# FFN down products issued in threes between the pair products

## The chip, the cores and the metric

The kernel runs on one core of one Trainium2 chip. The metric is the device time of one launch, in microseconds. TensorE is named PE (its weight loads PEld), VectorE DVE, ScalarE ACT, GpSimd POOL, and SyncE, which issues the loads, SP.

## The reference, cut to what matters

One transformer block on 512 tokens of 1024 features: a feed-forward network (FFN), an attention mixer, a second FFN, and a last norm. The change touches both FFNs alone.

```python
def swiglu(h, w_gate, w_up, w_down):
    return (jax.nn.silu(h @ w_gate) * (h @ w_up)) @ w_down

x = x + 0.5 * swiglu(rmsnorm(x, norm_ffn1[l]), w_ffn1_gate[l], w_ffn1_up[l], w_ffn1_down[l])
x = x + hybrid_mixer(rmsnorm(x, norm_mix[l]), ...)
x = x + 0.5 * swiglu(rmsnorm(x, norm_ffn2[l]), w_ffn2_gate[l], w_ffn2_up[l], w_ffn2_down[l])
```

`w_gate` and `w_up` are 1024 x 2816, `w_down` is 2816 x 1024, all float32.

## The kernel before, in words

Every matrix is held as a sum of a high and a low half, and every product of two 128-blocks is made of three matmuls (high by high, high by low, low by high): `mm3`, lines 100 to 103. In a trace each `mm3` is one row of L101, one of L102 and one of L103. The halves of a weight are made by ACT (high, L92 or L233) and DVE (low, L96 or L234).

An FFN has 22 feature blocks `f` of 128. The first four are computed plainly (`plain`, products called `pgu`). The other 18 are computed in nine pairs by a scheme with seven products instead of eight on half-width operands (`pair`, line 304). A pair has 14 steps: seven products (`u`, `v` or `w`) for gate and for up. A step is four `mm3` with 256 columns each, so 12 matmuls (`pu`, `pv`, `pw` in the trace). Each step needs a sum of weight tiles (L319, some steps), a high half (L233) and a low half (L234). Behind a step follow small sums out of PSUM (L339 to L365).

The products with `w_down` (`down`, line 385) go by groups of four feature blocks: for each of the eight output blocks `d`, four `mm3` with 512 columns, 12 matmuls called `pd`, accumulate in one PSUM bank, and `half_added` (L507, DVE) adds the half of it to `x[d]`. The down products of a group of four are laid between the pair steps of the next group of four (`mixed`, line 419): after about every fourth pair step, one block of 12 `pd` matmuls. The down products of the first, plain group stand ahead of the pairs, in two batches of four output blocks. The last group (two feature blocks, `f` 20 and 21) has 14 pair steps, between which seven of the eight blocks of `f` 16 to 19 lie, the eighth behind them. After it the first FFN has the down products of its last two feature blocks (`wd1b`), and the second FFN goes on with transposes of `x` (`px`) and the last products.

`go` (line 442) walks the list of steps in order. It issues a step's loads 12 steps ahead, its weight sums 6 ahead, its halves 4 ahead. The walk gives the order by priority; a list scheduler with a simulated timeline then fixes each engine's order, and may pass an instruction whose inputs are late in its simulation. `tc.issue_after(ins)` makes the instructions in its block stand behind `ins` on that engine's queue.

PSUM has eight banks, in four tags (`s`, `t`, `o`, `mm`) of two. `u` uses `s`, `v` uses `t`, `w` uses `o`; the blocks of down products between pairs use `mm`; the first group's down products take the tags in rotation (`pt` with tag `None`, line 48).

Of the kernel before, what the change touches and what calls it, by code (L numbers as in the profile page):

```python
# [18 lines left out]
NK = D // 128  # L19
NF = F // 128  # L20
NT = S // 128
FP = 4
# [7 lines left out]
def block_kernel(ctx: ExitStack, tc: tile.TileContext, A: dict, out: bass.AP):  # L30
# [7 lines left out]
    nc = tc.nc  # L38
# [9 lines left out]
    def pt(tag, name):  # L48

        if tag is None:  # L50
            tag = ("s", "t", "o", "mm")[turns[0] % 4]
            turns[0] += 1
        return ps.tile([128, S], F32, name=name, tag=tag, bufs=2)
# [46 lines left out]
    def mm3(p, w, v, first, last, again=False):  # L100
        nc.tensor.matmul(p, w[0], v[0], start=first, stop=False, skip_group_check=again)  # L101
        nc.tensor.matmul(p, w[0], v[1], start=False, stop=False, skip_group_check=again)  # L102
        nc.tensor.matmul(p, w[1], v[0], start=False, stop=last, skip_group_check=again)  # L103

    def mm2(p, w, v, first, last):

# [10 lines left out]
    for k in range(NK):  # L117
        x = xp.tile([128, S], F32, name=f"x{k}")
# [73 lines left out]
    class Ffn:  # L192
# [14 lines left out]
        def __init__(self, wg, wu, which, tmp, hp, sp):  # L207
            self.w, self.which, self.tmp, self.hp, self.sp = (wg, wu), which, tmp, hp, sp
            self.xg, self.hs, self.steps = None, {}, []
            self.b, self.temps = {}, {}  # L210
            self.last_lo = None
            self.x_made = None
            self.rms_at = {}
            self.th, self.tl = [sp.tile([128, 4, 3, HT], F32R, name=n, tag=n, bufs=1) for n in ("th3", "tl3")]
            sp.tile([128, 16], F32, name="gap", tag="gap", bufs=1)
# [88 lines left out]
        def pair(self, f):  # L304

            A, half, bank, part, out = {}, {}, {}, {}, {}
# [22 lines left out]
            def run(m, to, a, b, first):  # L329
                if first:  # L330
                    bank[m, to] = ps.tile([128, S], F32, name="p" + to, tag={"u": "s", "v": "t", "w": "o"}[to],
                                          bufs=2)[:, :HT]
                hi, lo = half.pop((m, a))
                for k, x in enumerate(self.moving(b)):
                    mm3(bank[m, to], (hi[:, k], lo[:, k]), x, first and k == 0, k == 3, not first)

            def copied(m, to, name):
                part[m, name] = self.sp.tile([128, HT], F32, name="wc", tag="wc", bufs=4)
# [43 lines left out]
                                  lambda m=m, then=then: then(m)])  # L382
            return steps

        def down(self, w, fs, then, tag="mm", groups=(1,) * NK, kept_back=True):

            n = len(fs)
            raw, got, bank = {}, {}, {}

            def loads(d):  # L390
                if d % (8 // n) == 0:
                    raw[d * n // 8] = chunk((8, 128))
                    fetch(raw[d * n // 8], w[d * n // 8])

            def halves_of(d):
                if d % (4 // n) == 0:
                    i = d * n % 8
                    with self.behind_lo() if kept_back else nullcontext():
                        parts = halves(raw[d * n // 8][:, i:i + 4])
                    for k, v in enumerate(parts):  # L400
                        got[d + k // n, k % n] = v

            def run(d):
                ds = {sum(groups[:g]): range(sum(groups[:g]), sum(groups[:g + 1])) for g in range(len(groups))}.get(d)
                if ds is None:
                    return
                for i in ds:
                    bank[i] = pt(tag, "pd")
                for ks in ([range(n)] if len(ds) == 1 else [range(n - 1), range(n - 1, n)]):
                    for i in ds:  # L410
                        for k in ks:
                            mm3(bank[i], got[i, k], self.hs[fs[k]], k == 0, k == n - 1)
                for i in ds:
                    then(i, bank[i])

            return [[lambda d=d: loads(d), None, lambda d=d: halves_of(d), lambda d=d: run(d), None, True]
                    for d in range(NK)]

        def mixed(self, steps, fills, tail=1):

# [8 lines left out]
        def lay(self, wd):  # L429

            for f in range(FP):
                self.steps += self.plain(f)
            self.steps += self.down(wd[0], range(FP), half_added, None, (4, 4), False)
            fills = []
            for f in range(FP, NF, FP):
                fs = range(f, min(f + FP, NF))
                pairs = [step for i in fs[::2] for step in self.pair(i)]
                self.steps += self.mixed(pairs, fills) if fills else pairs
                if len(fs) == FP:
                    fills = self.down(wd[f // FP], fs, half_added)  # L440

        def go(self, after):
            steps, at = self.steps, [0, 0, 0]
            late, count = None, 0
            for i, s in enumerate(steps):
                for j, ahead in enumerate((12, 6, 4)):
                    while at[j] < min(i + ahead + 1, len(steps)):
                        if steps[at[j]][j]:
                            steps[at[j]][j]()
                        at[j] += 1  # L450
                down = len(s) == 6
                if down and late:
                    late()
                s[3]()
                if not down:
                    if late:
                        late()
                    if i == 2 * FP - 1:
                        s[4]()
                        s[4] = None  # L460
                    after(count)
                    count += 1
                late = s[4]
            if late:
                late()


    scr_t = dp.tile([16, 128, RVW], F32, name="scr_t")
# [40 lines left out]
    with ExitStack() as ph:  # L509
        tmp = ph.enter_context(tc.tile_pool(name="tmp1", bufs=5))  # L510
        hp = ph.enter_context(tc.tile_pool(name="hp1", bufs=2))
        sp = ph.enter_context(tc.tile_pool(name="sp1", bufs=2))


        wake = pt(None, "wake")
        for _ in range(12):
            nc.tensor.matmul(wake.rearrange("p (a b) -> p a b", a=4), ones,
                             ones.unsqueeze(1).to_broadcast([128, 4, 128]), start=True, stop=True)
        nc.scalar.activation(R[:, 0:1], eps, AF.Sqrt)
        ffn = Ffn(A["wg1"], A["wu1"], 0, tmp, hp, sp)  # L520
        ffn.xg = [gained(k, 0) for k in range(NK)]
        ffn.x_made = made[0]
        ffn.rms_at = {(1, 0, 4): summed, (1, 1, 0): turned_R}

        make_rows = bias_rows(hp)

        def after(i):
            if i == 0:
                with tc.issue_after(ffn.first_up.ins):
                    for k in range(NK):  # L530
                        squares(hp, k, "h", 16)
                rms(None)
            if i == 3:
                make_rows()
            if 3 <= i < 7:
                ffn.sums_of_x(i - 3)
            if i == 7:
                for k in range(4):
                    ffn.blocks_of_x(k)
            if 20 <= i < 60 and i % 5 == 0:  # L540
                h = slice(2 * (i // 5) - 8, 2 * (i // 5) - 6)
                row = scr_r[h]
                with behind_fetched():
                    nc.sync.dma_start(scr_t[h].rearrange("h p w -> p h w"),
                                      bass.AP(tensor=row.tensor, offset=row.offset,
                                              ap=[[0, 128], [RVW, 2], [1, RVW]]))
            if i >= 70 and i % 8 == 0 and (i - 72) // 8 < 8:
                a = (i - 72) // 8
                row = scr_c[0:1, :]
                with behind_fetched():  # L550
                    for j in range(NT):
                        nc.sync.dma_start(
                            cb[a * 16:(a + 1) * 16, j],
                            bass.AP(tensor=row.tensor, offset=row.offset + 31 - 8 * j - a,
                                    ap=[[CMW, 16], [16 * CMW, 8], [1, 32]]))

        xg = []

        def then(d, p):
            if d == 0:  # L560
                with tc.issue_after(ffn.silu.ins):
                    nc.scalar.activation(rc[:, 0:1], eps, AF.Sqrt)
            half_added(d, p)
            xg.append(gained(d, 1))
            squares(tmp, d, "tmp", 5)

        ffn.lay(A["wd1a"])
        ffn.steps += ffn.down(A["wd1b"], range(NF - NF % FP, NF), then, None, (4, 2, 2))
        ffn.go(after)


    with ExitStack() as ph:
# [12 lines left out]
        got = {}  # L585
# [637 lines left out]
```

## Time and profile before

| | us |
|---|---|
| median of 3 runs | 998.72 (997.28 to 998.82) |
| profiled execution, its own time | 999.69 |
| its span, first to last instruction | 997.9 |
| PE busy | 979.2 (98%), 6084 matmuls |
| PEld busy | 870.7 (87%) |
| DVE busy | 780.9 (78%) |
| ACT busy | 566.3 (57%) |
| mean granted PE clock | 0.997 |

The pair stages of the two FFNs lie at about 70 to 340 us and 700 to 972 us of the span. Rows of a timeline carry a start and a duration, both in us; matmuls are pipelined, so a row's duration is longer than the time to the next row's start, and it is the distance of starts that adds up to the span.

### The profile page before, as it was taken

How to read it: one execution, taken by the hardware profiler on the slowest of the kernel's cores; microseconds unless marked ns; L12 is line 12 of the kernel's file. 1: busy time of each engine (PE TensorE's matmuls, PEld its weight loads, DVE VectorE, ACT ScalarE, POOL GpSimd, SP SyncE). 2: the span in 40 equal slices, each digit the busy share in tenths (PEclk: the TensorE clock that was granted, in tenths of full speed). 3: DMA queues.
4: the chain of work that ended last, by engine and by line, in shares of the span. 5: the costliest groups of instructions: out<-in, count | busy, mean ns of one | idle time of the engine just before them, and what ended most of it. 6: DMA issues, size and time to landing. Idle time of an engine off the chain costs nothing.

```text
span 997.9 us, 16910 instructions
## 1 busy us (share of the span) xinstructions
PE 979.2 (98%) x6084; PEld 870.7 (87%) x6084; DVE 780.9 (78%) x1579; ACT 566.3 (57%) x1165; POOL 132.6 (13%) x176
## 2 busy tenths in 40 slices
PE   9999999999999999999999999999999999999996
PEld 6789999999999898787877888888998999999995
DVE  6996987687777587768788978889788787777854
ACT  6464655454544365567687886656456455444426
POOL 0000000000000000035666666100000000000002
PEclk9999999999999999999999999999999999999999
DMA  7345544332321136531221232135343322341102
GB/s 258 104 172 175 190 128 132 109 98 82 108 66 50 51 97 186 171 114 33 61 62 54 80 86 79 64 99 197 89 165 114 118 78 76 127 127 43 54 11 85
DMA packets 50057, 104.52 MB, mean 105 GB/s; under 512 B 10130, under 2 KB 14691, under 8 KB 49973
## 3 DMA queue, kind: packets, MB, share of 16 engines
q1 hardware_dynamic: 49684, 102.91, 33.1%
q8 instruction: 48, 0.79, 0.3%
q10 hardware_dynamic: 288, 0.52, 0.1%
q14 instruction: 37, 0.30, 0.1%
HBM read 97.98 MB, written 5.30 MB: 103 GB/s over the span
## 4 chain that ended last, share of the span: by engine, by line
PE 92%; DVE 4%; ACT 1%; DMA 1%; issue 1%; SPq 0%; ACTq 0%; DVEq 0%
PE pd L101 8%; PE pd L102 8%; PE pd L103 8%; PE pu L101 6%; PE pu L103 6%; PE pu L102 6%; PE pw L101 5%; PE pw L102 4%; PE pw L103 4%; PE pp L103 3%; PE pgu L101 3%; PE pgu L102 3%; PE pp L101 3%; PE pgu L103 3%; PE pp L102 3%; PE pv L101 3%
## 5 line engine op out<-in xcount | busy, mean ns | idle before, releaser
L233 ACT ACTIVATE sph<-aw 128x512 fp32r<-128x512 f32 x252 | 157.7, 630 | 158.6 <-PE pu L102 74.6
L92 ACT ACTIVATE whi<-raw 128x512 fp32r<-128x512 f32 (+1 forms) x200 | 122.1, 621 | 174.7 <-PE pd L102 88.4
L234 DVE TENSOR_TENSOR spl<-aw,sph 128x512 fp32r<-128x512 f32 x252 | 170.8, 686 | 56.6 <-ACT sph L233 53.2
L102 PE MATMUL pd<-h,whi 128*128 128x512 f32 x336 | 131.5, 391 | 0.0
L96 DVE TENSOR_TENSOR wlo<-raw,whi 128x512 fp32r<-128x512 f32 (+1 forms) x168 | 111.2, 672 | 25.8 <-ACT whi L92 22.2
L103 PE MATMUL pd<-h,wlo 128*128 128x512 f32 x336 | 130.5, 389 | 0.0
L101 PE MATMUL pd<-h,whi 128*128 128x512 f32 x336 | 129.3, 392 | 0.0
L101 PE MATMUL pu<-th,sph 128*128 128x256 f32 x432 | 121.2, 281 | 0.0
L103 PE MATMUL pu<-th,spl 128*128 128x256 f32 x432 | 121.1, 280 | 0.0
L102 PE MATMUL pu<-tl,sph 128*128 128x256 f32 x432 | 121.1, 280 | 0.0
L319 DVE TENSOR_TENSOR aw<-aw 128x512 f32<-128x512 f32 x144 | 98.2, 683 | 0.0
L507 DVE SCALAR_TENSOR_TENSOR x<-pd,x 128x512 f32<-128x512 f32 x88 | 59.8, 685 | 40.2 <-PE pd L103 39.3
L102 PEld LDWEIGHTS pu<-tl,sph 128*128 128x128 f32 x432 | 82.0, 190 | 1.2
L101 PEld LDWEIGHTS pu<-th,sph 128*128 128x128 f32 x432 | 81.5, 189 | 1.1
L103 PEld LDWEIGHTS pu<-th,spl 128*128 128x128 f32 x432 | 81.2, 188 | 0.0
L101 PE MATMUL pw<-xo,sph 128*128 128x256 f32 x288 | 80.7, 281 | 0.0
L102 PE MATMUL pw<-xo,sph 128*128 128x256 f32 x288 | 80.5, 280 | 0.0
L103 PE MATMUL pw<-xo,spl 128*128 128x256 f32 x288 | 79.7, 280 | 0.0
L103 PEld LDWEIGHTS pd<-h,wlo 128*128 128x128 f32 x336 | 63.1, 188 | 12.9
L102 PEld LDWEIGHTS pd<-h,whi 128*128 128x128 f32 x336 | 63.3, 189 | 10.7
L101 PEld LDWEIGHTS pd<-h,whi 128*128 128x128 f32 x336 | 63.1, 188 | 11.0
L102 PEld LDWEIGHTS pw<-xo,sph 128*128 128x128 f32 x288 | 54.9, 190 | 1.1
(246 smaller groups left out, 2445.8 us busy)
## 6 DMA issues: line engine op xcount, KB each, us to landing
aw<-in_wg SPq DMA_DIRECT2D x72, 256.0 KB, 3.3
aw<-in_wu SPq DMA_DIRECT2D x72, 256.0 KB, 4.5
raw<-in_wd1a SPq DMA_DIRECT2D x20, 512.0 KB, 4.0
raw<-in_wd2a SPq DMA_DIRECT2D x20, 512.0 KB, 5.2
raw<-in_w_a SPq DMA_DIRECT2D x16, 512.0 KB, 4.5
raw<-in_w SPq DMA_DIRECT2D x8, 512.0 KB, 4.1
raw<-in_w_o SPq DMA_DIRECT2D x8, 512.0 KB, 3.5
raw<-in_wg SPq DMA_DIRECT2D x7, 512.0 KB, 4.0
```

The costliest lines, as they stand in the source:

```text
L92: last_hi[0] = nc.scalar.activation(hi, v, AF.Copy)
L96: nc.vector.tensor_tensor(lo, v, f32(hi), ALU.subtract)
L101: nc.tensor.matmul(p, w[0], v[0], start=first, stop=False, skip_group_check=again)
L102: nc.tensor.matmul(p, w[0], v[1], start=False, stop=False, skip_group_check=again)
L103: nc.tensor.matmul(p, w[1], v[0], start=False, stop=last, skip_group_check=again)
L233: nc.scalar.activation(hi, v, AF.Copy)
L234: self.last_lo = nc.vector.tensor_tensor(lo, v, f32(hi), ALU.subtract)
L319: nc.vector.tensor_tensor(to, x, y, op)
L507: nc.vector.scalar_tensor_tensor(xs[d], p, 0.5, xs[d], ALU.mult, ALU.add)
```

## The change

A block of down products between pair steps is no longer issued as 12 matmuls in a row. It is taken apart into four `mm3` (triples), which go to a list `waiting`. After each pair step one triple is issued; a second one goes into the middle of the step if more than four wait. Each triple's matmuls are ordered behind the last pair matmul issued so far (`in_pair`) with `issue_after`. `half_added` follows the block's last triple. Of the first group's down products, ahead of the pairs, all but the last triple are issued as before; the last one waits, and a counter `held` keeps it back for the first five pair steps and lets it out at the end of the sixth. The PSUM tags of that first group are now fixed by output block (`s`, `t`, `o`, `mm`). What still waits when the steps are over is issued in a row. `wd1b` keeps its order.

```diff
     def mm3(p, w, v, first, last, again=False):
...
-        nc.tensor.matmul(p, w[1], v[0], start=False, stop=last, skip_group_check=again)
+        return nc.tensor.matmul(p, w[1], v[0], start=False, stop=last, skip_group_check=again)
...
+            self.waiting = []
+            self.in_pair = None
+            self.held = 5
...
                 for k, x in enumerate(self.moving(b)):
-                    mm3(bank[m, to], (hi[:, k], lo[:, k]), x, first and k == 0, k == 3, not first)
+                    self.in_pair = mm3(bank[m, to], (hi[:, k], lo[:, k]), x, first and k == 0, k == 3, not first)
+                    if k == 1:
+                        self.between(self.held == 0 and len(self.waiting) > 4)
+                self.between(self.held == 0)
+                self.held = max(self.held - 1, 0)
...
-        def down(self, w, fs, then, tag="mm", groups=(1,) * NK, kept_back=True):
+        def down(self, w, fs, then, tags=("mm",), groups=(1,) * NK, kept_back=True, left=None):
...
-                for i in ds:
-                    bank[i] = pt(tag, "pd")
+
+                def triple(i, k):
+                    if k == 0:
+                        bank[i] = pt(tags[i % len(tags)], "pd")
+                    with tc.issue_after(self.in_pair.ins) if left != 0 and self.in_pair else nullcontext():
+                        mm3(bank[i], got[i, k], self.hs[fs[k]], k == 0, k == n - 1)
+                    if k == n - 1:
+                        then(i, bank[i])
+
+                todo = []
                 for ks in ([range(n)] if len(ds) == 1 else [range(n - 1), range(n - 1, n)]):
-                    for i in ds:
-                        for k in ks:
-                            mm3(bank[i], got[i, k], self.hs[fs[k]], k == 0, k == n - 1)
-                for i in ds:
-                    then(i, bank[i])
+                    todo += [lambda i=i, k=k: triple(i, k) for i in ds for k in ks]
+                at = 0 if left is None else len(todo) - (left if ds[-1] == NK - 1 else 0)
+                if at:
+                    self.between(len(self.waiting))
+                for one in todo[:at]:
+                    one()
+                self.waiting += todo[at:]
...
+        def between(self, n):
+
+            for _ in range(min(n, len(self.waiting))):
+                self.waiting.pop(0)()
...
-            self.steps += self.down(wd[0], range(FP), half_added, None, (4, 4), False)
+            self.steps += self.down(wd[0], range(FP), half_added, ("s", "t", "o", "mm"), (4, 4), False, 1)
...
             if late:
                 late()
+            self.between(len(self.waiting))
...
-        ffn.steps += ffn.down(A["wd1b"], range(NF - NF % FP, NF), then, None, (4, 2, 2))
+        ffn.steps += ffn.down(A["wd1b"], range(NF - NF % FP, NF), then, (None,), (4, 2, 2), left=0)
```

## Rows read from the trace of the kernel before

**Rows 1.** The page: the span, and each engine's busy time, share and instructions.
```profile
span 997.9 us, 16910 instructions
PE 979.2 (98%) x6084; PEld 870.7 (87%) x6084; DVE 780.9 (78%) x1579; ACT 566.3 (57%) x1165; POOL 132.6 (13%) x176
```

**Rows 2.** Stretches of the pair stages: length, busy time (instructions) by engine, granted clock.
```profile
core 0: us, PE busy (x) PEld busy (x) DVE busy (x) ACT busy (x) POOL busy (x), PEclk, DMA share, GB/s
141.25:339.72 198.47, 198.47 (x1369) 184.74 (x1368) 148.66 (x257) 95.13 (x179) 0.00 (x0) 1.00 0.29 86
773.60:972.07 198.47, 198.47 (x1369) 184.74 (x1368) 148.67 (x257) 93.66 (x177) 0.00 (x0) 1.00 0.25 79
700.60:753.90 53.30, 52.20 (x409) 50.52 (x408) 41.68 (x75) 27.49 (x56) 0.00 (x0) 1.00 0.38 119
```

**Rows 3.** The same stretch, PE's instructions that write `pd` alone.
```profile
141.25:339.72 198.47, 81.80 (x337) 1.00 0.29 86
```

**Rows 4.** Timeline of PE: a block, 72 pair matmuls, the next block (first of each).
```profile
144.09 0.40 PE L101 MATMUL pd<-h,whi 128*128 128x512 f32 x1
...
146.83 0.28 PE L101 MATMUL pv<-xo,sph 128*128 128x256 f32 x1
...
155.31 0.40 PE L101 MATMUL pd<-h,whi 128*128 128x512 f32 x1
```

**Rows 5.** Timeline of PE: two down matmuls, 44 pair matmuls, a block (first of each).
```profile
133.50 0.40 PE L101 MATMUL pd<-h,whi 128*128 128x512 f32 x1
...
133.97 0.28 PE L101 MATMUL pu<-th,sph 128*128 128x256 f32 x1
...
138.97 0.40 PE L103 MATMUL pd<-h,wlo 128*128 128x512 f32 x1
```

**Rows 6.** Groups by line, 141.25 to 339.72 us: busy us, mean ns of one.
```profile
L101 PE MATMUL pu<-th,sph 128*128 128x256 f32 x152 | 42.7, 281 | 0.0
```

**Rows 7.** The same view, 134.0 to 138.96 us.
```profile
L101 PE MATMUL pu<-th,sph 128*128 128x256 f32 x8 | 2.2, 277 | 0.0
```

**Rows 8.** Timeline: three down matmuls, 16 pair matmuls, the next down (first of each).
```profile
125.14 0.40 PE L102 MATMUL pd<-h,whi 128*128 128x512 f32 x1
...
125.84 0.28 PE L102 MATMUL pw<-xo,sph 128*128 128x256 f32 x1
...
127.66 0.40 PE L102 MATMUL pd<-h,whi 128*128 128x512 f32 x1
```

**Rows 9.** Timeline: four down, seven pair, one down, pair (first of each).
```profile
121.57 0.40 PE L103 MATMUL pd<-h,wlo 128*128 128x512 f32 x1
...
122.50 0.28 PE L101 MATMUL pw<-xo,sph 128*128 128x256 f32 x1
...
123.33 0.39 PE L101 MATMUL pd<-h,whi 128*128 128x512 f32 x1
123.56 0.28 PE L103 MATMUL pw<-xo,spl 128*128 128x256 f32 x1
```

**Rows 10.** Timeline: six pair, two down, 18 pair, then down (first of each).
```profile
700.57 0.28 PE L101 MATMUL pu<-xo,sph 128*128 128x256 f32 x1
...
701.28 0.40 PE L101 MATMUL pd<-h,whi 128*128 128x512 f32 x1
...
701.75 0.28 PE L101 MATMUL pu<-xo,sph 128*128 128x256 f32 x1
...
703.79 0.40 PE L103 MATMUL pd<-h,wlo 128*128 128x512 f32 x1
```

**Rows 11.** Timeline of PE: around its one stop in the second FFN's pairs.
```profile
749.62 0.28 PE L103 MATMUL pv<-xo,spl 128*128 128x256 f32 x1
751.00 0.39 PE L101 MATMUL pu<-xo,sph 128*128 128x256 f32 x1 [1.10 <-ACT t L361]
```

**Rows 12.** Timeline of ACT, same stretch.
```profile
749.01 0.63 ACT L92 ACTIVATE whi<-raw 128x512 fp32r<-128x512 f32 x1 [3.93 <-DMA raw<-in_wd2a]
```

**Rows 13.** Waits, 141.25 to 339.72 us: us in total, times, longest us.
```profile
ACT whi L92 <- PE pd L102: 39.7, 29, 2.1
DVE x L507 <- PE pd L103: 15.1, 12, 2.9
```

## The prediction

> **What bounds the kernel now.** The page comes first: PE is busy 979.2 of 997.9 us [rows 1]. Such a share can hide a slow issue, so the second view is the table of stretches. In 141.25 to 339.72 us PE is busy for all of 198.47 us, at a granted clock of 1.00, while DVE is busy 148.66 us and ACT 95.13 us; the second FFN's stretch has the same 198.47 us [rows 2]. So in these two stretches nothing but PE's own pace sets the time, and the change removes no matmul. The only stop above 1 us in the pair stages is at 749.62 us [rows 11].
>
> What can still move is how far apart PE starts its matmuls, so the third view is the timeline of PE, read by distances of starts. From 146.83 to 155.31 us there are 72 pair matmuls, 8.48 / 72 = 117.8 ns each [rows 4]. From 133.97 to 138.97 us there are 44 of the same shape, 5.00 / 44 = 113.6 ns each [rows 5]. The same product has two paces. The groups by line show it as well: one L101 `pu` takes 281 ns on average in the long stretch and 277 ns in the short one [rows 6, 7]. In both long stretches the pace is the slow one throughout.
>
> What decides between them, in this trace, is the run of `pd` matmuls just before. Behind a block of 12 the pace is slow [rows 4]. Behind two `pd` it is fast [rows 5], also where it was slow before: 6 pair matmuls in 0.71 us (118 ns), two `pd`, then 18 in 2.04 us (113.3 ns) [rows 10]. Behind three `pd` it is fast, 16 in 1.82 us (113.8 ns) [rows 8]. Behind four it is slow, 7 in 0.83 us (118.6 ns), and the next single `pd` leads to the fast pace again [rows 9]. I went through all such runs in both pair stages: 12 have one to three `pd` (three of one, six of two, three of three), and a fast pace follows each; 69 have four or more, and a slow pace follows each, six of them although it was fast before. What is not in the trace: three `pd` with a slow pace before them. All three cases of three came from the fast pace.
>
> **The change part by part.** The list of steps puts four triples into `waiting` at every fourth pair step, and each pair step lets one out at its end. So PE should see 12 pair matmuls, 3 `pd`, 12 pair matmuls and so on, with the second triple in the middle of a step only where more than four wait (at the turn of a group of four, and in all of the last 14 steps).
>
> *Pace of the pair matmuls.* Each long stretch holds 1369 PE instructions, 337 of them `pd` [rows 2, 3]; one `pd` is the tail of the block before, so 336 `pd` and 1032 pair matmuls. By triples all of these follow a run of three, so they go at 113.6 instead of 117.8 ns: 2 x 1032 x 4.2 ns = 8.7 us less. Check of the sum: 1032 x 117.8 ns = 121.6 us, and 198.47 - 121.6 = 76.9 us for 336 `pd`, 228.9 ns each, which agrees with 2.74 us / 12 = 228 ns of a block [rows 4].
>
> *Price of the triples.* A `pd` run is slower at its start. Three `pd` take 125.14 to 125.84 us, 0.70 us [rows 8]; three in a block take 3 x 228.9 = 687 ns. So each lone triple costs 13 ns more. There are 2 x 336 / 3 = 224 triples in the two stretches. By the counts of the list, 11 in each FFN still wait when the steps are over and go out in one row, which leaves 202 lone ones: 2.6 us more.
>
> *Sum for the two stretches:* -8.7 + 2.6 = -6.1 us.
>
> *The first pair steps* (from 70 and from 700 us). Part of their `pd` runs are short already, and part of the pace is fast already [rows 5, 8 to 10]. The one triple that is held back should bring the fast pace from the seventh step on. But there PE is not alone: at 749.62 us PE stops for 1.3 us, for a bank that ACT L361 frees, and ACT had stood 3.93 us for a load of `w_down` [rows 11, 12]. A faster PE reaches this wait earlier and waits longer; the load comes when the tiles of the weight sums are free, which the change leaves alone. I take 0 here. Bounds: below, the stop goes (-1.3) and some 340 pair matmuls of 700.60 to 753.90 us at the slow pace [rows 2] turn fast (-1.4), with as much in the first FFN, -4.1 in all; above, a second such stop, +1.3.
>
> *Order edges.* `issue_after` orders PE behind PE and I cost it at nothing; the trace has no row of it alone. Below nothing it cannot go, since an order adds no speed but the one counted; above, the nearest row is the distance between a slow and a fast matmul, 4.2 ns, times 224 = 0.9 us.
>
> *`half_added` and the halves of `w_down`.* `half_added` follows the fourth triple, and DVE has waited up to 2.9 us for `pd` already without stopping PE [rows 13]; DVE is busy 148.66 of 198.47 us [rows 2], so its work stays hidden. ACT's L92 waits for `pd` L102, which releases the buffer of halves: 39.7 us over 29 times, the longest 2.1 us [rows 13]. With triples a buffer is held over four steps instead of one block, and high halves of the pair weights stand behind L92 in ACT's queue. There are five such buffers and about two blocks live at a time, so I cost this at nothing. If the cover went, PE would stand for one L92 wait, up to 2.1 us, per group of four (three per FFN): +12.6 us as the far end, which I hold unlikely, for PE leaves ACT 0.52 of the stretch idle.
>
> *Bank tags and the end.* The first group's tags free `s` first, which the pairs need first; the second FFN had that order by rotation, and PE shows no stop at either start: 0. At the end 33 `pd` in a row instead of 12 stand before `px` or `wd1b`; the products are the same and the last pair's values get more time: 0.
>
> **Forecast.** The profiled execution took 999.69 us (span 997.9 and 1.8 around it). 999.69 - 6.1 = 993.6. It lay 1.0 above the median, so the median should fall from 998.7 to 992.7 us.
>
> **A rule that speaks against it.** The rows first: 117.8 and 113.6 ns for one shape at one granted clock [rows 4, 5]. The Trainium skill, page "TensorE: Matmul & The Clock Gate", section "Back-to-back issue gap", gives one spacing per width, 262 cycles for 256 columns, which at 2.4 GHz is 109.2 ns. By that rule the order of widths is free, and the change would give nothing. This trace shows neither that value nor a single one. It is the rival below on order without effect.
>
> **Rivals.**
> - *Slower: the triple counts as a block.* If three `pd` coming from the slow pace leave PE slow, as four do [rows 9], no step ever turns fast, and each triple still costs 13 ns: +2.6 us, 1001.3. Its place is the third `pd` of the triple, and it decides at the first lone triple of each FFN, since all later ones inherit the pace. For it: no such case is in the trace. Against it: one and two `pd` from the slow pace lead to the fast one [rows 5, 9, 10], and three keep it [rows 8].
> - *Order without effect.* The paces come from something else that goes along with the run lengths (which operands, which DVE work). Then -8.7 falls away; with the starts of runs no dearer either, 998.7. Against it: pace changes at the run, within one step.
> - *Half of it.* The edge holds a triple from below only. Where the scheduler's simulation finds it late, two triples meet, six `pd` make a run, and the next step is slow. With half of the steps so: -4.3 us and some 1.5 us for the run starts, 995.9. For it: early in the second group the old order is scattered by single matmuls [rows 8, 9]. Against it: from 141 us on it is regular.
> - *More than forecast.* The first steps give what their lower bound says: -6.1 - 4.1, 988.5.
>
> **How the numbers follow.** Forecast 0.58, more 0.12, half 0.12, without effect 0.06, slower 0.12. A measurement of this kernel tells about 0.2%, 2.0 us, from no change. Faster: 0.58 + 0.12 + 0.09 of the half case = 0.79; same: 0.03 + 0.06 = 0.09; slower 0.12. The range goes from 989.0 to 999.5: it holds the forecast, the half case, the case without effect and part of the larger gain, about 0.83; the slower case stays outside.
>
> **What would show it.** In the changed kernel's groups by line, the pair matmuls of the long stretches should have a mean of 276 to 277 instead of 281 ns. The timeline should show `pd` in threes, about 0.70 us each, between twelves of 1.36 us, and the two stretches should be shorter by about 3 us each. The stop near 750 us should still be there. The forecast is wrong if the mean stays 281 ns behind runs of three, if runs of six or more are common, or if PE shows new stops for `sph`, `spl` or a bank.

## The result and the profile after

The changed kernel takes 991.97 us (median of 6 runs, 990.21 to 993.91), the kernel before 997.46 (6 runs, 996.53 to 998.82). The ratio is 0.9941, with a 95% interval of 0.993 to 0.9953: 5.5 us less, where the prediction had 6.1. The profiled executions are 990.21 and 999.69 us; those two lie 9.5 apart, and the steps below say which part of that is the change.

The changed kernel's page, with the columns of [rows 1]: PE does the same 6084 matmuls and is as full as before, with 8.7 us less busy time.

```profile
span 988.4 us, 16902 instructions
PE 970.5 (98%) x6084; PEld 859.0 (87%) x6084; DVE 778.5 (79%) x1579; ACT 561.9 (57%) x1165; POOL 132.5 (13%) x176
```

Two stretches of its pair stages, with the columns of [rows 2]. The second fence holds the instructions that write or read `pd` alone, in the first stretch: busy time (instructions) of PE, of its weight loads and of DVE.

```profile
130.00:331.60 201.60, 201.60 (x1422) 186.37 (x1422) 152.86 (x268) 97.40 (x187) 0.00 (x0) 1.00 0.30 94
755.70:957.20 201.50, 201.50 (x1421) 186.24 (x1420) 152.64 (x267) 95.88 (x185) 0.00 (x0) 1.00 0.27 89
```

```profile
130.00:331.60 201.60, 97.27 (x339) 55.53 (x339) 19.56 (x29) 1.00 0.30 94
```

PE is still busy throughout at a granted clock of 1.00. The first stretch holds 339 `pd` and 1083 pair matmuls. At the distances of before (228.9 and 117.8 ns, [rows 2 to 4]) these would take 205.2 us; they take 201.60, 3.6 less. So the gain lies in the distance of starts. The groups by line of the first stretch show the mean of a pair matmul, which answers to [rows 6]:

```profile
L101 PE MATMUL pu<-th,sph 128*128 128x256 f32 x161 | 44.4, 276 | 0.0
```

276 ns instead of 281. The timeline of PE shows the new order (first of each):

```profile
124.33 0.40 PE L101 MATMUL pd<-h,whi 128*128 128x512 f32 x1
124.56 0.40 PE L102 MATMUL pd<-h,whi 128*128 128x512 f32 x1
124.80 0.39 PE L103 MATMUL pd<-h,wlo 128*128 128x512 f32 x1
125.03 0.28 PE L103 MATMUL pw<-xo,spl 128*128 128x256 f32 x1
...
126.16 0.40 PE L101 MATMUL pd<-h,whi 128*128 128x512 f32 x1
...
126.86 0.28 PE L101 MATMUL pu<-th,sph 128*128 128x256 f32 x1
...
128.22 0.40 PE L101 MATMUL pd<-h,whi 128*128 128x512 f32 x1
```

Three `pd` take 0.70 us (124.33 to 125.03), as in [rows 8], and twelve pair matmuls 1.36 us (126.86 to 128.22), 113.3 ns each. The slow pace of [rows 4] is gone from this stretch, but for the two pair matmuls behind its one run of six `pd`.

### The profile page after: what moved, and what is told of

It is laid out like the page before. It is cut to its first block, busy times and chain, and to the rows that moved or that the text cites. A ratio compares the mean times of both kernels' runs of the same rounds, so it can differ in the third digit from the quotient of the medians.

```text
span 988.4 us, 16902 instructions
## 1 busy us (share of the span) xinstructions
PE 970.5 (98%) x6084; PEld 859.0 (87%) x6084; DVE 778.5 (79%) x1579; ACT 561.9 (57%) x1165; POOL 132.5 (13%) x176
## 4 chain that ended last, share of the span: by engine, by line
PE 91%; DVE 4%; issue 1%; ACT 1%; DMA 1%; POOL 0%; SPq 0%; POOLq 0%; ACTq 0%; DVEq 0%
PE pd L102 8%; PE pd L103 8%; PE pd L101 8%; PE pu L101 6%; PE pu L103 6%; PE pu L102 6%; PE pw L101 4%; PE pw L103 4%; PE pw L102 4%; PE pp L103 3%; PE pp L101 3%; PE pp L102 3%; PE pgu L102 3%; PE pgu L101 3%; PE pgu L103 3%; PE ps_t L940 3%
## 5 line engine op out<-in xcount | busy, mean ns | idle before, releaser
L102 PE MATMUL pu<-tl,sph 128*128 128x256 f32 x432 | 119.2, 276 | 0.0
L101 PE MATMUL pw<-xo,sph 128*128 128x256 f32 x288 | 79.7, 277 | 0.2 <-ACT sph L236 0.2
L102 PE MATMUL pw<-xo,sph 128*128 128x256 f32 x288 | 79.5, 276 | 0.0
```

## The experiments

The theory: the run of `pd` just ahead decides the pace. One to three lead to 113.4 ns a pair matmul, four or more to 117.8. The rivals: even spreading alone does it (less crowding of buffers, of weight loads or of DVE); the price of a triple is something else; or the pace hangs on the operands. "Pair matmuls" are those with 256 columns, `pd` those with 512. Paces and counts of runs below are sums over distances of starts in the traces. Each kernel is a change to the changed kernel, if nothing else is said; each ratio is against runs of the kernel before that were taken beside it.

**The changed kernel and its near kin.** First a bare chain of matmuls, in which runs of wide ones from 1 to 12 stand between narrow ones:

```
for n, count in SEGS:          # (256, 24), (512, k), (256, 24), ...
    for _ in range(count):
        ...
        nc.tensor.matmul(banks[n][:, :n], wr[:, i], x[:, :n], start=True, stop=True)
```

> The kernel leaves out the whole block: it only runs chains of matmuls on 128-row operands that are loaded once, with no work of DVE or ACT beside them: 24 matmuls of 256 columns, then k of 512 columns, then 24 of 256 again, with k of 1, 2, 3, 4, 5, 6, 8 and 12, once coming from the slow pace (behind 12 of 512) and once from the fast one (behind 2 of 512). Theory (the run length of the wide matmuls sets the pace): 113.4 ns per 256-column matmul behind k of 1 to 3, 117.8 ns behind k of 4 and more, whatever the pace before; three from the slow pace lead to the fast one. Rival (operands, or DVE and ACT work beside them, set the pace): one pace everywhere here. Rival (three from the slow pace count as a block): fast behind three only where it was fast before. Behind 11 wide, 1 to 3 narrow, 1 wide the theory expects the fast pace as well.

It took 368.5 us. Apart from the start of the list, where the scheduler mixed the two widths, the runs of 1 to 12 stand in the trace as listed. One line of its groups:

```profile
L54 PE MATMUL p<-x,wr 128*128 128x256 f32 x1797 | 230.2, 283 | 0.0
```

283 ns is above both means of the kernel (276 and 281), and by distances of starts the 24 narrow ones behind each run were 119.0 to 120.1 ns apart, whatever its length. That is the rival's forecast, one pace everywhere, and it is a third pace, met again below. But all these matmuls read one moving tile, which the kernel's do not.

> The changed kernel again, as the yardstick on this chip: 0.994 of the kernel before, about 992 us.

The changed kernel again: 990.69 us against 998.63, ratio 0.9931 [0.9907, 0.9955]. The gain is there again.

Two triples together behind every second step (still spread over the whole FFN, but in runs of six; the scheduler made 68 of them and left 22 blocks of twelve):

```
-                    if k == 1:
-                        self.between(self.held == 0 and len(self.waiting) > 4)
-                self.between(self.held == 0)
+                self.turn = not self.turn
+                if self.held == 0 and self.turn:
+                    self.between(4 if len(self.waiting) > 5 else 2)
```

> The changed kernel, but two triples go out together behind every second pair step, so that down matmuls come in runs of six, still spread evenly. Theory (run length sets the pace): the pair matmuls of the long stretches go back to 117.8 ns, 2 x 1032 x 4.2 = 8.7 us more, a six costs 14 ns less than two triples, 1.4 us less: about 7 us above the changed kernel, 999 us, as the kernel before. Rival (even spreading for DVE, ACT and PSUM is what helps): within 1 us of the changed kernel, 992 us.

999.7 us, ratio 1.0011 [1.0, 1.0022]: the whole gain is gone. Its timeline, and one line of its groups from 140 to 330 us:

```profile
202.17 0.40 PE L101 MATMUL pd<-h,whi 128*128 128x512 f32 x1
...
203.56 0.28 PE L101 MATMUL pu<-th,sph 128*128 128x256 f32 x1
...
204.97 0.28 PE L101 MATMUL pv<-xo,sph 128*128 128x256 f32 x1
```

```profile
L101 PE MATMUL pu<-th,sph 128*128 128x256 f32 x144 | 40.5, 281 | 0.0
```

Behind six `pd` (1.39 us), twelve pair matmuls take 1.41 us, 117.5 ns, and the mean is 281 again. All 66 runs of six that met the slow pace left it slow. Behind four runs of five it was slow for the first three pair matmuls alone. So spreading alone isn't it.

No triple held back and no order edge for the first group (`left` 1 becomes 0 for the first four feature blocks):

```
-            self.steps += self.down(wd[0], range(FP), half_added, ("s", "t", "o", "mm"), (4, 4), False, 1)
+            self.steps += self.down(wd[0], range(FP), half_added, ("s", "t", "o", "mm"), (4, 4), False, 0)
```

> The changed kernel, but the first group's last triple is not held back: all of that group goes out ahead of the pairs. Theory: the first 28 pair steps of each FFN have no lone triple and stay slow until a stop or the second group's first triples turn them: at most 2 x 22 x 12 x 4.2 ns = 2.2 us more; part of it is taken back at the stops for the loads of the down weights; I expect 1 us more, 993 us. Rival (the first steps are bound by loads and ACT anyway): no difference, 992 us.

992.81 us, 0.9942 [0.9921, 0.9962]. It overlaps the interval of the changed kernel, so in time it tells nothing. In the trace the stretch of the first 336 pair matmuls, stops and the `pd` between them included, takes 46.82 us in the second FFN against 45.69 in the changed kernel run beside it, and 47.18 against 47.15 in the first. In the second FFN, with no triple to turn the pace, all 361 pair matmuls from 709.61 to 752.13 us are slow (117.8 ns). In the first it turned fast at 99.12 us by itself, with no `pd` there and no distance above 124 ns. So the held triple is worth about 1 us in one FFN and nothing in the other, in these two traces.

**Run length alone, and short runs without spreading.** The chain again, in a forced order, with the operands split into high and low parts as the kernel's are:

```
-            last = nc.tensor.matmul(banks[n][:, :n], wr[:, i], x[:, :n], start=True, stop=True)
+            with tc.issue_after(last.ins) if last else nullcontext():
+                last = nc.tensor.matmul(bank[n][:, :n], w[part == 2][:, b], x[part == 1][:, :n], start=True, stop=True)
```

> Leaves out the whole block; chains of matmuls alone, in a fixed order, with high and low operands taken as in the kernel (high by high, high by low, low by high; four moving blocks, several weight tiles) and no work of DVE or ACT beside them. 24 matmuls of 256 columns stand before and behind k of 512 columns, k of 1, 2, 3, 4, 5, 6, 9, 12, from the slow and from the fast pace; then 12 and 3, 48 and 12, 12 and 6 in turn. Theory (run length alone): 113.4 ns behind k of 1 to 3, 117.8 ns behind 4 and more, also behind sixes. Rival (run length decides only where operands lie as in the kernel, since the first chains, on one moving operand, went at about 120 ns everywhere): one pace or other values here, without the step between 3 and 4.

295.25 us. The timeline behind a run of two wide ones, followed by 24 narrow:

```profile
39.90 0.40 PE L56 MATMUL p<-lo,hi 128*128 128x512 f32 x1
40.14 0.40 PE L56 MATMUL p<-hi,lo 128*128 128x512 f32 x1
40.37 0.28 PE L56 MATMUL p<-hi 128*128 128x256 f32 x1
...
43.23 0.40 PE L56 MATMUL p<-hi 128*128 128x512 f32 x1
```

2.86 / 24 = 119.2 ns behind a run of two, and between 119.0 and 120.1 ns behind every run from 1 to 12. As a law for any matmuls, the theory fell in both chains: length alone doesn't give 113.4.

In the kernel, then, with nothing spread out. A block of twelve is cut so that a short run ends it. Nine in a row, three pair matmuls, three more `pd`:

```
-                    if k == 1:
-                        self.between(self.held == 0 and len(self.waiting) > 4)
-                self.between(self.held == 0)
+                    if k == 0:
+                        self.between(self.held == 0 and len(self.waiting))
...
-                at = 0 if left is None else len(todo) - (left if ds[-1] == NK - 1 else 0)
+                at = len(todo) - (1 if left is None else left if ds[-1] == NK - 1 else 0)
```

> Blocks of down products are laid as in the kernel before, nine matmuls in a row, but the block's last triple goes out behind the first three pair matmuls of the next step. Theory (the run just before sets the pace; spreading is not needed): the pair matmuls behind the lone triple go at 113.4 ns, only those between nine and three and those behind the few whole twelves are slow; a block costs 36 ns less in its run starts than four lone triples; about the changed kernel's time, 0.5 us less, 990 us. Rival (even spreading): as the kernel before, 998 us.

992.63 us, 0.9953 [0.9937, 0.997]. Its timeline (first of each):

```profile
200.30 0.40 PE L101 MATMUL pd<-h,whi 128*128 128x512 f32 x1
...
202.37 0.28 PE L101 MATMUL pu<-th,sph 128*128 128x256 f32 x1
202.49 0.28 PE L102 MATMUL pu<-tl,sph 128*128 128x256 f32 x1
202.60 0.28 PE L103 MATMUL pu<-th,spl 128*128 128x256 f32 x1
202.72 0.40 PE L101 MATMUL pd<-h,whi 128*128 128x512 f32 x1
...
203.42 0.28 PE L101 MATMUL pu<-th,sph 128*128 128x256 f32 x1
...
205.80 0.28 PE L101 MATMUL pv<-xo,sph 128*128 128x256 f32 x1
```

Nine `pd`, three pair matmuls in 0.35 us (117 ns), three `pd`, then 21 in 2.38 us, 113.3 ns. All 48 lone triples that met the slow pace turned it fast, and behind 46 of 46 runs of nine it was slow. That is the case that was missing ahead of the prediction, and most of the gain comes without even spreading. The scheduler left 14 blocks whole, and the slow pace keeps 21% of the pair matmuls.

Eleven, three pair matmuls, one (the last product of a block goes out by itself):

```
+                        if left is None and k == n - 1 and part < 2:
+                            w, v = got[i, k], self.hs[fs[k]]
+                            if part == 0:
+                                nc.tensor.matmul(bank[i], w[0], v[0], start=False, stop=False)
+                                nc.tensor.matmul(bank[i], w[0], v[1], start=False, stop=False)
+                            else:
+                                nc.tensor.matmul(bank[i], w[1], v[0], start=False, stop=True)
```

> The same with eleven in a row and one single matmul behind the first three pair matmuls of the next step. Theory: one wide matmul turns the pace as three do, at 50 ns less a block than four lone triples; the slow pair matmuls in between give some of it back: 1.4 us under the changed kernel, 989.5 us. Rival (even spreading): 998 us. Rival (one wide matmul does not turn it after three slow ones): 997 us.

991.26 us, 0.9943 [0.9928, 0.9958]. One `pd` was enough 48 times of 48. `pd` costs 229.2 ns on average here, against 232.3 in the changed kernel, since there are fewer starts of longer runs; the slow pace keeps 22% of the pair matmuls, again with 14 whole blocks.

All `pd` between the pairs but the last product of each block as two halves of 256 columns (both halves start sums in one bank, which changes the values of `pd`):

```
+        two = slice(0, S // 2), slice(S // 2, S)
+        for b in two:
+            nc.tensor.matmul(p[:, b], w[0], v[0][:, b], start=first, stop=False, skip_group_check=True)
...
+        for b in (slice(0, S),) if last else two:
+            nc.tensor.matmul(p[:, b], w[1], v[0][:, b], start=False, stop=last, skip_group_check=True)
```

> The changed kernel, but the down matmuls between the pairs are taken as two of 256 columns each, but for the last one of every block of 12, which stays 512 wide and turns the pace once a block. Theory (the starts of wide runs and the pace behind them are all that differs): a wide matmul in a triple takes 232 ns, two narrow ones at the fast pace 227 ns; 350 of them in each FFN, less 10 ns a block for the lone wide one: 3 us under the changed kernel, 987.5 us. Rival (a narrow stream with twice the weight loads falls to the slow pace): 2 x 117.8 = 236 ns for each, and slow pairs: about 1000 us.

1005.17 us, 1.0081 [1.0066, 1.0096], 18 us off what I expected. Its timeline (first of each):

```profile
199.80 0.40 PE L110 MATMUL pd<-h,whi 128*128 128x256 f32 x2
200.04 0.40 PE L112 MATMUL pd<-h,wlo 128*128 128x256 f32 x2
200.28 0.28 PE L101 MATMUL pw<-xo,sph 128*128 128x256 f32 x1
...
201.70 0.40 PE L108 MATMUL pd<-h,whi 128*128 128x256 f32 x2
...
202.18 0.39 PE L112 MATMUL pd<-h,wlo 128*128 128x512 f32 x1
202.41 0.28 PE L101 MATMUL pu<-th,sph 128*128 128x256 f32 x1
...
203.77 0.40 PE L108 MATMUL pd<-h,whi 128*128 128x256 f32 x2
```

A pair of halves takes 0.24 us, 120 ns each, and leaves the pair matmuls slow: 12 in 1.42 us (200.28 to 201.70). One `pd` of 512 columns at the end of a block, and the next 12 take 1.36 us. So a narrow `pd` takes 120 ns where a pair matmul of the same shape takes 113.3 or 117.8, runs of them leave the pair matmuls slow, and one wide `pd` turns the pace. A narrow `pd` differs in several ways from a pair matmul: other weights and values, the same weights loaded twice in a row, the halves of a bank in turn. This run doesn't tell which of them counts; that the pace hangs on the operands was my guess here.

**What of the operands.** The chain again, now as sums of several matmuls in one bank:

```
-                                        start=True, stop=True)
+                                        start=kind == 0 or c < kind, stop=kind == 0 or c >= count - kind,
+                                        skip_group_check=True)
```

> Leaves out the whole block; the chains of the second such kernel, which went at 119.7 ns behind every run length, once more, but with sums kept in PSUM as in the kernel: the first matmul of a run starts a sum and the others add to it. Two stretches go without sums (kind 0), one writes the two halves of a bank in turn (kind 2). Theory (the pace behind wide runs shows only where matmuls add to the same columns of a bank, as pair matmuls do): 113.4 ns behind 1 to 3 wide ones, 117.8 ns behind 4 and more, and 120 ns without sums or with halves in turn. Rival (something else of the kernel decides, such as DVE and ACT beside it or where operands lie): 120 ns throughout, as before.

239.62 us, and 283 ns as the mean of each narrow group; 119 to 120 ns by distances of starts. Summing isn't what the chain lacked.

Eleven and one, with an edge that keeps the pair matmuls behind the eleven (`wide` is the last of them), so that no block stays whole, timed against the changed kernel itself:

```
-                    self.in_pair = mm3(bank[m, to], (hi[:, k], lo[:, k]), x, first and k == 0, k == 3, not first)
+                    with tc.issue_after(self.wide.ins) if self.wide else nullcontext():
+                        self.in_pair = mm3(bank[m, to], (hi[:, k], lo[:, k]), x, first and k == 0, k == 3, not first)
+                    self.wide = None
```

> As the kernel with eleven in a row and one behind three pair matmuls, but the next step's first three pair matmuls are also ordered behind the eleven, so that no block falls together into twelve. Theory: behind every single one the pair matmuls go at 113.4 ns; the slow share of them falls from 0.22 to about 0.1; down matmuls at 229.2 instead of 231.9 ns or more, 1.3 us less in each FFN than with triples, 0.4 us more for the slow pair matmuls in between: 1.8 us under the changed kernel, about 989 us. Rival (the gain of the pace is used up, other stops take over): the changed kernel's time, 991 us.

> The changed kernel once more, on the chip and beside the runs of the version with eleven and one: 0.994 of the kernel before, about 991 us.

990.67 us, 0.9927 [0.9914, 0.994], and 991.7 us, 0.9935 [0.9921, 0.9949]. The eleven-and-one version has the lowest ratio of all, 1.0 us below the changed kernel in the medians where 1.8 was expected, but the intervals overlap: that it beats the changed kernel is not shown. The pace was fast behind 62 of 62 single `pd`.

Last, the changed kernel without a tile of 64 bytes per partition that nothing reads or writes. It is made in the pool of `sph` and `spl`, ahead of them, and stands in the kernel before too; the order of the instructions in the FFNs stays:

```
-            sp.tile([128, 16], F32, name="gap", tag="gap", bufs=1)
```

> The changed kernel without its unused tile of 64 bytes per partition (name gap) that lies ahead of the pairs' weight halves in memory: the same instructions in the same order in the FFNs, but these weight tiles lie 64 bytes lower against the moving tiles. Theory (run length sets the pace only where the operands lie as here; elsewhere it is 120 ns, as in the chains of matmuls alone): the pair matmuls go at about 120 ns behind triples too, 2 x 1512 x 6.4 ns = 19 us more, 1010 us. Rival (the place of the operands does not matter, the chains lack something else of the kernel): 113.5 ns and 991 us.

1006.74 us, 1.0084 [1.0067, 1.01]. One line of its groups from 140 to 330 us, and its timeline:

```profile
L101 PE MATMUL pu<-th,sph 128*128 128x256 f32 x144 | 40.6, 282 | 0.0
```

```profile
203.17 0.40 PE L101 MATMUL pd<-h,whi 128*128 128x512 f32 x1
...
203.87 0.28 PE L101 MATMUL pu<-th,sph 128*128 128x256 f32 x1
...
205.29 0.40 PE L101 MATMUL pd<-h,whi 128*128 128x512 f32 x1
```

Three `pd`, and then twelve pair matmuls in 1.42 us where the changed kernel needs 1.36. All 230 lone triples are followed by this pace, 119.1 ns on average, the one of the bare chains. PE's 6084 matmuls stand in the same order in both traces. By the code the change moves the tiles made behind the unused one (`aw`, `sph`, `spl`, `wc`); the traces hold no addresses. So the same order with these tiles moved by 64 bytes loses 15 us, and the whole effect of the runs with them.

## Why the prediction was right

*Pace of the pair matmuls, -8.7.* Measured -9.15: the last 1032 pair matmuls of each FFN take 121.54 us before and 116.97 after (117.8 and 113.3 ns). The difference is mostly that of 113.3 to the 113.6 ns of [rows 5].

*Price of the triples, +2.6.* Measured +3.06 over all `pd`: they take 120.69 and 109.85 us in the two FFNs before, 122.10 and 111.50 after. 13 ns a lone triple was right (0.70 us against 0.687). But 230 of them stand in the trace where I counted 202: 106 in each FFN behind its first 480 pair matmuls, and 9 ahead of them, where now too the `pd` come in threes.

*Sum for the two stretches, -6.1.* Measured -9.15 + 3.06 = -6.1. That it agrees to 0.1 us is in part luck: both terms came out larger, and the second one is of all `pd`. With 212 x 13 ns = 2.8 us for the stretches alone the sum is about -6.4.

*The first pair steps, 0.* The first 480 pair matmuls, stops included, changed by +0.5 us in the first FFN (55.52 to 55.99) and by -2.0 in the second (57.41 to 55.38), inside the bounds of -4.1 to +1.3. Two things met here that I had costed together. The pace turned fast earlier, as the lower bound had it. The stops moved: in the second FFN the sum of stops fell from 1.38 to 0.50 us, in the first it rose from 0.22 to 1.30. I had said that the stop near 750 us should stay. On the changed kernel's timeline it comes earlier and is shorter, and two new ones stand in the first FFN:

```profile
108.21 0.28 PE L102 MATMUL pw<-xo,sph 128*128 128x256 f32 x1
108.68 0.38 PE L101 MATMUL pw<-xo,sph 128*128 128x256 f32 x1 [0.19 <-ACT sph L236]
108.90 0.28 PE L102 MATMUL pw<-xo,sph 128*128 128x256 f32 x1
109.47 0.39 PE L101 MATMUL pu<-th,sph 128*128 128x256 f32 x1 [0.29 <-ACT wc L346]
```

```profile
743.38 0.28 PE L102 MATMUL pv<-xo,sph 128*128 128x256 f32 x1
743.88 0.39 PE L101 MATMUL pu<-xo,sph 128*128 128x256 f32 x1 [0.22 <-ACT t L368]
744.10 0.28 PE L102 MATMUL pu<-xo,sph 128*128 128x256 f32 x1
...
749.87 0.40 PE L101 MATMUL pd<-h,whi 128*128 128x512 f32 x1
```

From 743.38 to 743.88 us is 0.50 us, 0.38 above the usual distance, and it waits for the same line as in [rows 11] (L361 there, L368 here). The new ones wait for a high half of the weights (`sph`) and for a copy out of PSUM (`wc`), both made by ACT. A new stop for `sph` was among the prediction's signs of being wrong; it came, too small to move the sum. So in the first steps PE does stop for ACT as feared, but the sums of stops differ from profile to profile (2.56 us in the first FFN of the second repeat of the changed kernel), and only their order of size, about 1 us, can be told.

*Order edges, `half_added` and the halves, tags and end, each 0.* None shows as a term of its own. ACT's wait for `pd` and DVE's wait, which answer to [rows 13], became shorter in the stretch from 130.00 to 331.60 us, in the columns of that view:

```profile
ACT whi L92 <- PE pd L102: 15.6, 13, 1.7
DVE x L531 <- PE pd L103: 9.1, 8, 1.8
```

The far end of +12.6 us for the halves did not come: 39.7 us of waiting became 15.6.

*From the stretches to the time.* From the first pair matmul to PE's first matmul behind the FFN it is 2.7 us less in the first; to the last matmul it is 5.1 less in the second; the attention between them is 1.6 less. That last part isn't the change's: the kernel before has a granted clock of 0.79 from 404 to 412 us, the changed kernel 1.00, and its second repeat 0.79 again. The three views, in that order:

```profile
404.00:412.00 8.00, 6.56 (x33) 5.53 (x32) 6.36 (x15) 4.49 (x10) 0.00 (x0) 0.79 0.59 181
```

```profile
404.00:412.00 8.00, 8.00 (x47) 6.94 (x46) 5.76 (x11) 4.91 (x10) 0.00 (x0) 1.00 0.83 275
```

```profile
404.00:412.00 8.00, 7.65 (x37) 6.70 (x38) 5.05 (x13) 3.89 (x8) 0.00 (x0) 0.79 0.69 221
```

Of the 9.5 us between the two profiles, 1.6 lie there and 1.6 in the first pair steps with their stops. That leaves 6.3, near the 6.1 of the stretches. Both other parts differ from one profile of the same kernel to the next, and the medians scatter too: 5.5, 7.9 and 6.5 us less in three measurements.

*What decides between the paces.* The prediction said: the run of `pd` just before. For the matmuls right behind a run this held, and it carried the forecast. (Of the 69 longer runs, seven and not six came from the fast pace.) But the pace is a state that changes without `pd` too, and the walk through the runs, which looked at what follows each, missed that. In the kernel before, 220 pair matmuls with no `pd` among them begin slow (117.8 ns to 98.85 us) and end fast (67 in 7.59 us, 113.3 ns), with a small stop between:

```profile
81.18 0.28 PE L103 MATMUL pv<-xo,spl 128*128 128x256 f32 x1
...
98.85 0.38 PE L101 MATMUL pw<-xo,sph 128*128 128x256 f32 x1
99.07 0.28 PE L102 MATMUL pw<-xo,sph 128*128 128x256 f32 x1
99.19 0.31 PE L101 MATMUL pu<-xo,sph 128*128 128x256 f32 x1
99.33 0.28 PE L102 MATMUL pu<-xo,sph 128*128 128x256 f32 x1
...
106.92 0.40 PE L101 MATMUL pd<-h,whi 128*128 128x512 f32 x1
```

In the changed kernel the pace was slow behind the stop at 743.38 us: the 49 pair matmuls from 744.10 to 749.87 us (fence above) take 117.8 ns each, until the next triple. The stop at 749.62 us of the kernel before [rows 11] changed nothing, slow before and behind it. So at a stop the pace can turn either way or stay, while behind one to three `pd` it was always fast, as long as the unused tile was there. Long runs had exceptions beside the fives above: in the first version with eleven and one, the six pair matmuls behind one run of 64 `pd` went at the fast pace.

*The rivals.* "The triple counts as a block" fell at its own point: the trace of the changed kernel has five lone triples that met the slow pace (one of them behind the stop at 743.38 us), the version with nine and three 48 more, and all led to the fast one. "Half of it" fell too; six `pd` in a row occur twice. "Order without effect" is wrong for this kernel, and the rule behind it (the Trainium skill, "TensorE: Matmul & The Clock Gate", section "Back-to-back issue gap": 262 cycles at 256 columns, 109.2 ns) matches no run here: the same shape at a granted clock of 1.00 had 113.4, 117.8 and about 119.5 ns. That section of the Trainium skill calls its 262 cycles the gap of an isolated matmul and says that in a stream with weight loads both instructions set the spacing; the prediction read it too widely. The rival had a point all the same: something else than the run length does matter. With the tiles 64 bytes lower, no run turned the pace.

What stays open: which tile's place decides and by what, and why PE comes out of a short run of wide matmuls, or of a stop, in one pace or the other. No run here separates these.

## What to carry to other kernels

Where PE is full for a long stretch, compare distances of starts between groups of one shape before counting its time as fixed: 4 ns a matmul were 9 us here. Follow the pace through whole stretches, too, and not only behind the event that you suspect: here it turned at stops as well. What stands ahead in the order can be the lever, and a kernel in which a single short run turns the pace needs no even spreading. Try such an order in the kernel itself and try it again after every change of its tiles, since 64 bytes of placement were worth more than the order.

## What I had not expected of the hardware

- One matmul shape (128 x 256, the weights loaded for each) had three paces at a full granted clock: 113.4, 117.8 and 119 to 120 ns. The last was the only one in bare chains, whatever ran ahead.
- An unused tile of 64 bytes per partition is worth 15 us of 992.
- The pace persists: 361 pair matmuls in a row were slow where no short run came (709.61 to 752.13 us of the version without a held triple), and at small stops it turned either way.
- `pd` pays at the start of a run: a lone triple is 233.3 ns each, a block of twelve 228.9 ns.
- Wide matmuls cut in halves were no cheaper: 2 x 120 ns against 229 to 233 ns for one of 512 columns.
